# Running the first token block alone and first, gathering part of the expert rows early, and turning the up projection round

## The chip, the cores and the metric

One core of a Trainium2 chip runs the kernel. The metric is the device time of one execution in microseconds; lower is better.

## The reference

One decoder block over 512 tokens of width 2048, in float32: a mixer (one input projection, half of it causal spatial gating in chunks of 128 tokens, half of it attention over a window of 128 tokens with sinks, one output projection) and then a channel mixer that picks, for every token and each of 8 heads, 16 of 16384 experts.

```python
h = rmsnorm(x, norm1_g);  z = h @ w_in
a_out = chunked_spatial_gating(gelu(zu), gelu(zv), ...)      # chunks of 128 tokens
b_out = sliding_window_attention(zq, zk, zvv, attn_sinks)    # window of 128
x = x + concatenate([a_out, b_out]) @ w_out
h2 = rmsnorm(x, norm2_g)
# peer(h2): 8 heads, top 16 of 128 x 128 product keys
q = h2 @ w_query;  s1, s2 = q1 @ sub_keys[0].T, q2 @ sub_keys[1].T
experts, gates = top16(top16(s1) + top16(s2)), softmax       # 128 experts for a token
a = gelu(einsum('cd,chkd->chk', h2, expert_down[experts]))
x = x + einsum('chk,chkd->cd', gates * a, expert_up[experts])
out = rmsnorm(x, norm_f_g)
```

## The kernel before

All matrix products are float32 made of three float32r products: an operand is split into a high part (a cast) and a low part (the rest), and `mm3` issues high x high, high x low and low x high. Weights come as 1 MiB chunks [128, 2048] in the order of their use. `Stream` loads them from SP into two buffers (`wraw`), casts each half on ScalarE (ACT) to `whi` and subtracts it on VectorE (DVE) or, where `on_pool` says so, on GpSimd (POOL) to `wlo`; each half is a *piece*, four pieces fit, and a piece is made two pieces ahead of its use. The request for a chunk stands in SP's queue behind the second split of the chunk that held its buffer.

The program runs in this order, and every engine takes its instructions in the order in which they are written:

1. The mixer for all four blocks of 128 tokens: `kT` and `vT`, eight tiles of queries, `v` by rows, eight tiles of `u` with attention and gating spread between (`attend`, `gate`), `mix`, the output projection (`project`, chunks of `wout`), second norm.
2. Queries of the channel mixer (`wq`) and the choice of experts (`choose`: top 16 on VectorE), spread by `fill`, a queue of small jobs of which every `tick` takes some.
3. The experts. The first three blocks (`TD` = 384 tokens) are computed densely, against all 16384 experts: `down` steps (128 experts each, h2 against a chunk of `down`, 48 matmuls of 384 columns, weights stationary) and `up` steps (eight groups of experts, 288 matmuls of 512 columns, the activations `gah`, `gal` stationary and the weights moving). What was not chosen has gate 0. The gates come from a table that is built with one-hot products (`table`, `quad`: tiles `eq`, `p`, `low`, `stage`) during the first 51 `down` steps (`OPEN`) and goes through DRAM (`g_dram`); activations of the first 56 steps go through `a_dram`. `make_ga` multiplies and splits them.
4. The fourth block is not dense: its 128 tokens' expert rows are gathered, 512 halves of 512 KB (one row of 4 KB for each token; indirect DMA from GpSimd, `fetch`, four buffers), and VectorE takes a dot product with each (`unit`, table down) or adds it with its weight (table up). These 512 units begin when `start_gather` runs, in the tenth tick after the 51 `down` steps, and are paced evenly over the rest.

The change rewrites the whole of this plan inside one function; the lines that a step of the prediction needs stand in the diff below.

## Time and profile before

| | us |
|---|---|
| runs | 3041.81, 3042.4, 3045.75; median 3042.4 |
| span of the profiled execution, first to last instruction | 3046.2 |
| TensorE busy | 2939.4 (96%) |
| VectorE busy | 2228.9 (73%) |
| ScalarE busy | 1095.9 (36%) |
| GpSimd busy | 1220.4 (40%) |
| DMA moved | 696.85 MB, 229 GB/s on average |

The stretches of the program on this time line: the first matmuls start at about 23 us; the mixer to the output projection ends at 582; queries and choice end at 786; the 51 `down` steps with the tables last from 786 to 1338; from there to the end come 77 `down` and 16 `up` steps, the first seven `up` steps nearly on end (1380 to 1852), with the gather beside them. A busy TensorE is not a full one: matmuls overlap, and what one costs is read from the distance of two starts.

### The profile page before, as it was taken

How to read it: one execution, taken by the hardware profiler on the slowest of the kernel's cores; microseconds unless marked ns; L12 is line 12 of the kernel's file. 1: busy time of each engine (PE TensorE's matmuls, PEld its weight loads, DVE VectorE, ACT ScalarE, POOL GpSimd, SP SyncE). 2: the span in 40 equal slices, each digit the busy share in tenths (PEclk: the TensorE clock that was granted, in tenths of full speed). 3: DMA queues.
4: the chain of work that ended last, by engine and by line, in shares of the span. 5: the costliest groups of instructions: out<-in, count | busy, mean ns of one | idle time of the engine just before them, and what ended most of it. 6: DMA issues, size and time to landing. Idle time of an engine off the chain costs nothing.

```text
span 3046.2 us, 38888 instructions
## 1 busy us (share of the span) xinstructions
PE 2939.4 (96%) x15021; PEld 2623.7 (86%) x15021; DVE 2228.9 (73%) x3266; ACT 1095.9 (36%) x1699; POOL 1220.4 (40%) x754
## 2 busy tenths in 40 slices
PE   7999999999989888999999999999999999999998
PEld 6888878799989888898788889898998989899896
DVE  3125642359998999967888887878888888888864
ACT  3244432222236655643323233232322323232333
POOL 2132100334435555633344344545445454554522
PEclk9999999999999999999999999999999999999999
DMA  5221242322334444569888888998989898898953
GB/s 188 90 82 57 70 166 88 120 83 84 110 115 159 155 168 160 195 250 350 302 312 333 328 304 316 328 328 311 331 312 339 312 336 314 318 340 314 338 212 132
DMA packets 193866, 696.85 MB, mean 229 GB/s; under 512 B 16528, under 2 KB 81296, under 8 KB 148240
## 3 DMA queue, kind: packets, MB, share of 16 engines
q1 hardware_dynamic: 104960, 378.04, 35.0%
q0 software_dynamic: 73728, 268.47, 24.4%
q10 hardware_dynamic: 14992, 47.86, 4.0%
q8 instruction: 118, 1.93, 0.3%
q14 instruction: 68, 0.56, 0.1%
HBM read 650.78 MB, written 43.52 MB: 228 GB/s over the span
## 4 chain that ended last, share of the span: by engine, by line
PE 49%; DVE 20%; issue 15%; POOL 10%; ACT 3%; DMA 2%; ACTq 0%; POOLq 0%; SPq 0%; DVEq 0%
POOL row L879 10%; PE dn L133 5%; PE acc L131 5%; PE dn L132 5%; PE dn L131 5%; PE acc L133 5%; PE acc L132 5%; PE up L132 5%; PE up L131 5%; PE up L133 5%; DVE wlo L112 4%; DVE stage L754 3%; DVE eq L719 2%; DVE cand L572 1%; PE tr L339 1%
## 5 line engine op out<-in xcount | busy, mean ns | idle before, releaser
L110 ACT CAST whi<-wraw 128x1024 fp32r<-128x1024 f32 x628 | 639.7, 1048 | 738.9 <-DMA wraw<-in_up 321.1
L112 DVE TENSOR_TENSOR wlo<-wraw,whi 128x1024 fp32r<-128x1024 f32 x550 | 719.5, 1312 | 252.9 <-ACT whi L110 251.9
L133 PE MATMUL dn<-h2d,wlo 128*128 128x384 f32 x2048 | 695.2, 339 | 28.8 <-DVE wlo L112 25.6
L131 PE MATMUL dn<-h2d,whi 128*128 128x384 f32 x2048 | 694.0, 339 | 8.4 <-ACT whi L110 8.4
L132 PE MATMUL dn<-h2d,whi 128*128 128x384 f32 x2048 | 692.3, 338 | 0.0
L131 PE MATMUL up<-whi,gah 128*128 128x512 f32 x1536 | 598.9, 390 | 3.2 <-DVE acc L978 3.0
L132 PE MATMUL up<-wlo,gah 128*128 128x512 f32 x1536 | 598.8, 390 | 3.0 <-DVE wlo L112 3.0
L133 PE MATMUL up<-whi,gal 128*128 128x512 f32 x1536 | 598.3, 390 | 0.0
L879 POOL DMA_INDIRECT row<-in_down_rows,idx x256 | 367.6, 1436 | 492.0 <-DVE row L894 470.2
L879 POOL DMA_INDIRECT row<-in_up_rows,idx x256 | 364.7, 1425 | 366.4 <-DVE half_row L901 345.5
L133 PEld LDWEIGHTS dn<-h2d,wlo 128*128 128x128 f32 x2048 | 388.1, 190 | 37.3 <-DVE wlo L112 33.1
L112 POOL TENSOR_TENSOR wlo<-wraw,whi 128x1024 fp32r<-128x1024 f32 x78 | 194.9, 2519 | 559.0 <-ACT whi L110 559.0
L131 PEld LDWEIGHTS dn<-h2d,whi 128*128 128x128 f32 x2048 | 388.5, 190 | 10.5 <-ACT whi L110 10.1
L132 PEld LDWEIGHTS dn<-h2d,whi 128*128 128x128 f32 x2048 | 388.4, 190 | 0.4
L131 PEld LDWEIGHTS up<-whi,gah 128*128 128x128 f32 x1536 | 288.8, 188 | 65.9 <-DVE acc L978 4.7
L132 PEld LDWEIGHTS up<-wlo,gah 128*128 128x128 f32 x1536 | 288.6, 188 | 63.3 <-DVE wlo L112 4.4
L133 PEld LDWEIGHTS up<-whi,gal 128*128 128x128 f32 x1536 | 288.8, 188 | 60.0
L901 DVE SCALAR_TENSOR_TENSOR half_row<-row,wgt,half_row 128x1024 f32<-128x1024 f32 x256 | 328.9, 1285 | 14.8 <-DMA row<-in_up_rows,idx 11.7
L894 DVE SCALAR_TENSOR_TENSOR row<-row,half_row 128x1024 f32<-128x1024 f32 x256 | 307.1, 1215 | 18.9 <-DMA row<-in_down_rows,idx 17.3
L722 POOL TENSOR_TENSOR p<-eq,gT 128x1024 fp32r<-128x1024 bf16 x96 | 236.2, 2468 | 206.9 <-DVE eq L719 196.0
L978 DVE TENSOR_TENSOR acc<-up,acc 128x512 f32<-128x512 f32 x192 | 129.3, 690 | 92.5 <-PE up L133 92.3
L951 ACT ACTIVATE aa<-dn 128x384 f32<-128x384 f32 x72 | 35.4, 492 | 348.2 <-PE dn L133 348.2
(194 smaller groups left out, 3441.6 us busy)
## 6 DMA issues: line engine op xcount, KB each, us to landing
wraw<-in_down SPq DMA_DIRECT2D x128, 1024.0 KB
wraw<-in_up SPq DMA_DIRECT2D x128, 1024.0 KB
wraw<-in_win SPq DMA_DIRECT2D x26, 1024.0 KB
g_dram<-stage ACTq DMA_DIRECT2D x24, 1024.0 KB
g<-g_dram SPq DMA_DIRECT2D x32, 768.0 KB
wraw<-in_wout SPq DMA_DIRECT2D x16, 1024.0 KB
wraw<-in_wq SPq DMA_DIRECT2D x16, 1024.0 KB
aa<-a_dram SPq DMA_DIRECT2D x56, 192.0 KB
```

Source lines behind the costliest of these rows:

```text
L110: self.nc.scalar.copy(hi, src)
L112: eng.tensor_sub(lo, src, hi.bitcast(F32))
L131: nc.tensor.matmul(ps, wh, xh, start=start, stop=False)
L132: nc.tensor.matmul(ps, wh, xl, start=False, stop=False)
L133: nc.tensor.matmul(ps, wl, xh, start=False, stop=stop)
L719: nc.vector.tensor_tensor(eq, iota[:, None, :].to_broadcast([P, 4, P]), t[:, 1, four, None].to_broadcast([P, 4, P]), op=OP.is_equal)
L722: nc.gpsimd.tensor_tensor(p2, eq[:, :, None, :].to_broadcast([P, 4, 2, P]), hl[:, four, :, None].to_broadcast([P, 4, 2, P]), op=OP.mult)
L754: nc.vector.tensor_tensor(stage[h][:, :, o:o + 4], ps[:, :, 0, k].rearrange("p t k -> p k t"), low[:, :, k].rearrange("p t k -> p k t"), o ...
L879: nc.gpsimd.indirect_dma_start(out=t, out_offset=None, in_=src, in_offset=bass.IndirectOffsetOnAxis(ap=idx[:, j, h:h + 1], axis=0))
L894: nc.vector.scalar_tensor_tensor(t, t, 1.0, half, op0=OP.mult, op1=OP.mult, accum_out=dots[:, j, h:h + 1])
L901: nc.vector.scalar_tensor_tensor(half, t, wgt[:, j:j + 1], half, op0=OP.mult, op1=OP.add)
L978: nc.vector.tensor_add(y, ps[b], y)
```

## The change

The first block of tokens becomes the gathered one, and runs through the whole mixer and its choice of experts before the other three begin. The weights of the mixer and of `wq` are therefore read and split twice: `wrow` (26 chunks), `wout` and `wq` (16 each) for block 0, tokens stationary and weights moving, and then again for blocks 1 to 3. The last 64 of the 512 tokens (`EX`) are gathered too, as 64 x 2 partitions with 256 further units; the dense part falls from 384 to 320 tokens. The gather is a `Flow` that `mm3` itself steps, at a rate for each part of the program (one unit in 2300 ns, 4500 ns, 3600 ns of matmul time, then evenly). Running sums and inputs of the gather pass through DRAM (`h_dram`, `y_dram`, `x_dram`). The `up` steps now keep the weights stationary and move the 320 activations, so that the result is transposed and has to be turned at the end (`rows_out`). Which splits GpSimd makes follows a rule of the piece's number.

```diff
-TD = ND * P
+TL = ND * P
+EX = 64
+TD = TL - EX
...
+    def step(self, ns):
+        if not self.q:
+            return
+        self.credit = min(self.credit + ns * self.rate, 3.0)
+        while self.q and self.credit >= 1.0:
+            self.credit -= 1.0
+            self.q.popleft()()
...
-    chunks = [a["win"][i] for i in range(26)]
-    chunks += [a["wout"][i] for i in range(16)]
-    chunks += [a["wq"][i] for i in range(16)]
+    lead = [a["wrow"][i] for i in range(26)] + [a["wout"][i] for i in range(16)]
+    lead += [a["wq"][i] for i in range(16)]
+    chunks = lead + [a["win"][i] for i in range(10)] + [a["wrow"][i] for i in range(10, 18)]
+    chunks += [a["win"][i] for i in range(10, 18)]
+    chunks += [a["wout"][i] for i in range(16)] + [a["wq"][i] for i in range(16)]
...
-    W.on_pool = [range(0, 4), range(20, 36), range(2 * 42 - 2, 2 * 70)]
+    def on_pool(p):
+        if p < 84:
+            return p % 4 == 1 and p > 4
+        if p < 116:
+            return p % 4 != 0
+        if p < 200:
+            return p % 2 == 0
+        if p < 232:
+            return p % 4 != 0
+        if p < 232 + 2 * OPEN:
+            return p % 2 == 0
+        return p % 3 == 0
...
+    def row_group(x, width, evac, every=2, budget=0.0):
+        ps = acc_tile()
+        n = 1024 // width
+        for i in range(KT // n):
+            hi, lo = W.get()
+            for k in range(n):
+                kt = i * n + k
+                c = slice(k * width, (k + 1) * width)
+                mm3(ps[:, :width], (x[0][:, kt, :], x[1][:, kt, :]), (hi[:, c], lo[:, c]),
+                    kt == 0, kt == KT - 1)
+            if kt == KT - 1:
+                evac(ps)
+            after_piece(every, budget)
...
+    counts = (P, EX)
+    units = [(i, src, h, j) for i, n in enumerate(counts) for src in (n_down, n_up)
+             for h in range(2) for j in range(n)]
...
-            ps = [late["ps"].tile([P, 512], F32, name="up", bufs=4) for _ in range(ND)]
+            ps = [late["ps"].tile([P, TD], F32, name="up", bufs=4) for _ in range(4)]
...
-                hi, lo = ga[CB * c + j]
-                mm3(ps[b], (hi[:, t], lo[:, t]), (w[0][:, k], w[1][:, k]), j == 0, j == CB - 1)
+            def multiply(m, j, w):
+                k = (j % 2) * 512 + m * P
+                x = ga[CB * c + j]
+                mm3(ps[m], (w[0][:, k:k + P], w[1][:, k:k + P]), x, j == 0, j == CB - 1)
...
+            w = [W.get(1), W.get(2)]
+            for m in range(4):
+                for j in range(4, 8):
+                    multiply(m, j, w[j // 2 - 2])
+                y = accT[:, 4 * q + m, :]
+                if c == 0:
+                    nc.scalar.copy(y, ps[m])
+                else:
+                    nc.vector.tensor_add(y, ps[m], y)
...
+    def pace():
+        left = sum(2 * 24 for k, i in order if k == "d" and i >= OPEN)
+        left += sum(384 for k, i in order if k == "u")
+        flow.rate = len(flow.q) / (left * TD * COL_NS - 40e3)
```

The order of instructions at three places. First VectorE while the tables are built; `eq` and `p` are one-hot tiles, `stage` takes the products, `wlo` is the split of a piece, `row` a gathered tile. Before:

```order
L754 TENSOR_TENSOR stage<-tr,low 128x64x4 x2
L719 TENSOR_TENSOR eq<-iota,eT 128x512
L112 TENSOR_TENSOR wlo<-wraw,whi 128x1024
L754 TENSOR_TENSOR stage<-tr,low 128x64x4 x2
L719 TENSOR_TENSOR eq<-iota,eT 128x512
L726 TENSOR_TENSOR p_9886<-iota,eT 128x512
```

and now:

```order
L972 TENSOR_TENSOR eq<-iota,eT 128x512
L119 TENSOR_TENSOR wlo<-wraw,whi 128x1024
L614 SCALAR_TENSOR_TENSOR row,dots_85<-row,half_row 128x1024
L1007 TENSOR_TENSOR stage<-tr,low 128x64x4 x2
L972 TENSOR_TENSOR eq<-iota,eT 128x512
L1007 TENSOR_TENSOR stage<-tr,low 128x64x4 x2
L972 TENSOR_TENSOR eq<-iota,eT 128x512
L979 TENSOR_TENSOR p_10398<-iota,eT 128x512
```

The dot products with gathered rows (`L614`), which stood behind the tables, now stand among them, some ninety in the 51 `down` steps, and one split of a chunk's two is left on VectorE.

Second GpSimd in the tail, between two stretches of the same length. Before, only requests for gathered rows stand there:

```order
L879 DMA row_22803<-in_up_rows,idx_3983 128x1024
L879 DMA row_22843<-in_up_rows,idx_3983 128x1024
L879 DMA row_22875<-in_up_rows,idx_3983 128x1024
L879 DMA row_22878<-in_up_rows,idx_3983 128x1024
L879 DMA row_22920<-in_up_rows,idx_3983 128x1024
```

and now:

```order
L601 DMA row_15787<-in_up_rows,idx0_79 128x1024
L119 TENSOR_TENSOR wlo_15816<-wraw_15675,whi_15815 128x1024
L601 DMA row_15829<-in_up_rows,idx0_79 128x1024
L601 DMA row_15856<-in_up_rows,idx0_79 128x1024
L601 DMA row_15880<-in_up_rows,idx0_79 128x1024
L119 TENSOR_TENSOR wlo_15887<-wraw_15739,whi_15886 128x1024
L601 DMA row_15912<-in_up_rows,idx0_79 128x1024
```

Every third piece is split here, and the requests for rows queue with the splits.

Third TensorE at the start of an `up` step. Before, with 512 weight columns moving past 128 tokens:

```order
L131 MATMUL up_11380<-whi_11293,gah_11127 128x512
L132 MATMUL up_11380<-wlo_11294,gah_11127 128x512
L133 MATMUL up_11380<-whi_11293,gal_11128 128x512
L131 MATMUL up_11381<-whi_11293,gah_11127 128x512
L132 MATMUL up_11381<-wlo_11294,gah_11127 128x512
```

and now, with 320 tokens moving past 128 weight columns:

```order
L143 MATMUL up_12728<-gah_12465,whi_12641 128x320
L144 MATMUL up_12728<-gal_12466,whi_12641 128x320
L145 MATMUL up_12728<-gah_12465,wlo_12642 128x320
L143 MATMUL up_12729<-gah_12465,whi_12641 128x320
L144 MATMUL up_12729<-gal_12466,whi_12641 128x320
```

The two operands changed places; an `up` step has 384 matmuls of 320 columns in place of 288 of 512.

## Rows read from the trace of the kernel before

**Rows 1.** Stretches: length; busy (count) of PE, PEld, DVE, ACT, POOL; clock; DMA share, GB/s.

```profile
56.30:388.90 332.60, 331.62 (x1685) 267.88 (x1685) 130.08 (x231) 126.80 (x263) 70.56 (x32) 1.00 0.23 80
388.90:581.90 193.00, 186.21 (x820) 149.03 (x818) 71.25 (x82) 56.43 (x89) 7.05 (x9) 1.00 0.34 126
581.90:786.50 204.60, 198.87 (x1119) 188.40 (x1120) 144.32 (x566) 57.62 (x78) 84.60 (x36) 0.99 0.25 88
786.50:1337.60 551.10, 497.66 (x2845) 480.44 (x2844) 510.77 (x730) 301.83 (x583) 290.62 (x118) 0.97 0.45 156
...
1337.60:3046.20 1708.60, 1690.52 (x8305) 1505.78 (x8303) 1352.95 (x1641) 529.50 (x657) 749.67 (x529) 1.00 0.86 310
...
1778.00:2908.00 1130.00, 1129.25 (x5715) 1027.46 (x5714) 932.56 (x1064) 342.85 (x413) 561.88 (x396) 1.00 0.90 323
```

**Rows 2.** Timeline of TensorE in three places: start, length, line, operation, tiles, shape.

```profile
23.12 0.28 PE L133 MATMUL acc<-hT,wlo 128*128 128x256 f32 x1
23.23 0.28 PE L131 MATMUL acc<-hT,whi 128*128 128x256 f32 x1
...
1860.26 0.34 PE L133 MATMUL dn<-h2d,wlo 128*128 128x384 f32 x1
1860.43 0.34 PE L131 MATMUL dn<-h2d,whi 128*128 128x384 f32 x1
...
1500.17 0.39 PE L131 MATMUL up<-whi,gah 128*128 128x512 f32 x1
1500.40 0.39 PE L132 MATMUL up<-wlo,gah 128*128 128x512 f32 x1
```

**Rows 3.** Groups of instructions of VectorE and GpSimd in the table stretch, 786.5 to 1337.6.

```profile
L112 DVE TENSOR_TENSOR wlo<-wraw,whi 128x1024 fp32r<-128x1024 f32 x80 | 141.3, 1766 | 28.1 <-ACT whi L110 27.7
L754 DVE TENSOR_TENSOR stage<-tr,low 128x256 f32<-128x256 f32 x192 | 107.8, 607 | 3.9 <-ACT low L751 3.9
L719 DVE TENSOR_TENSOR eq<-iota,eT 128x512 bf16<-128x512 f32 x96 | 94.9, 998 | 0.0
L726 DVE TENSOR_TENSOR p<-iota,eT 128x512 fp32r<-128x512 f32 x33 | 29.3, 888 | 0.0
...
L722 POOL TENSOR_TENSOR p<-eq,gT 128x1024 fp32r<-128x1024 bf16 x96 | 236.2, 2468 | 206.9 <-DVE eq L719 196.0 <-PE tr L738 7.8 <-PE tr L702 3.2
L112 POOL TENSOR_TENSOR wlo<-wraw,whi 128x1024 fp32r<-128x1024 f32 x22 | 54.5, 2501 | 60.5 <-ACT whi L110 60.5
```

**Rows 4.** Groups of instructions of VectorE from 1380 to 2908.

```profile
L112 DVE TENSOR_TENSOR wlo<-wraw,whi 128x1024 fp32r<-128x1024 f32 x371 | 452.6, 1220 | 14.2 <-ACT whi L110 13.6 <-issue 0.6
L901 DVE SCALAR_TENSOR_TENSOR half_row<-row,wgt,half_row 128x1024 f32<-128x1024 f32 x247 | 317.4, 1285 | 14.7 <-DMA row<-in_up_rows,idx 11.7 <-ACT half_row L892 0.4
L894 DVE SCALAR_TENSOR_TENSOR row<-row,half_row 128x1024 f32<-128x1024 f32 x256 | 307.1, 1215 | 18.9 <-DMA row<-in_down_rows,idx 17.3 <-ACT half_row L892 1.4
L978 DVE TENSOR_TENSOR acc<-up,acc 128x512 f32<-128x512 f32 x180 | 121.1, 690 | 78.4 <-PE up L133 78.2
L864 DVE TENSOR_TENSOR gal<-aa,gah 128x384 fp32r<-128x384 f32 x116 | 64.9, 559 | 69.1 <-ACT gah L863 69.1
```

**Rows 5.** Stretches as in rows 1, around one chunk that SP requests at 198.30.

```profile
198.30:199.20 0.90, 0.90 (x5) 0.72 (x5) 0.87 (x2) 0.00 (x0) 0.00 (x0) 1.00 0.00 0
199.20:203.00 3.80, 3.80 (x18) 3.04 (x17) 2.34 (x4) 1.69 (x3) 0.00 (x0) 1.00 0.80 276
```

**Rows 6.** Timelines of SP's queue and of ScalarE: a loaded chunk's request, its casts.

```profile
1524.78 6.03 SPq L100 DMA_DIRECT2D wraw<-in_up  x2
...
1532.51 2.00 ACT L110 CAST whi<-wraw 128x1024 fp32r<-128x1024 f32 x2 [6.24 <-DMA wraw<-in_up]
```

**Rows 7.** Stretches as in rows 1, two of the best 20 us of DMA.

```profile
1460.00:1480.00 20.00, 20.00 (x90) 16.54 (x89) 16.25 (x24) 4.11 (x4) 10.61 (x8) 1.00 1.02 406
...
1660.00:1680.00 20.00, 20.00 (x90) 16.57 (x89) 16.06 (x24) 4.11 (x4) 9.44 (x7) 1.00 1.02 401
```

**Rows 8.** The page's costliest groups: GpSimd's requests for rows.

```profile
L879 POOL DMA_INDIRECT row<-in_up_rows,idx x256 | 364.7, 1425 | 366.4 <-DVE half_row L901 345.5 <-DVE wlo L112 7.5 <-DVE row L894 5.9
```

More of the change, by code (lines that the diff above doesn't have):

```diff
@@ L110, in make @@
             self.nc.scalar.copy(hi, src)
-            eng = self.nc.gpsimd if any(p in r for r in self.on_pool) else self.nc.vector
+            eng = self.nc.gpsimd if self.on_pool(p) else self.nc.vector
             eng.tensor_sub(lo, src, hi.bitcast(F32))
@@ new lines, in block_kernel @@
+    row_group(hT0, 512, lambda ps: nc.scalar.activation(v0[:, 512:], ps, AF.Gelu))
+    rest = layernorm(plab, v0, lng0, lnb0)
+    nc.scalar.dma_start(gbc, bcast(a["norm2_g"], D))
+    rest()
+    row_group(hT0, 512, lambda ps: nc.scalar.activation(u0[:, :512], ps, AF.Gelu))
+    soon.append([lambda: gate_rows(0)])
+    soon.append([lambda: turn_gated(0)])
+    row_group(hT0, 512, lambda ps: nc.scalar.activation(u0[:, 512:], ps, AF.Gelu), every=1)
+    while soon:
+        for f in soon.popleft():
+            f()
@@ new lines, in block_kernel, with decode_first @@
+    for g in range(4):
+        qr = pdec.tile([P, 512], F32, name="qr")
+        if g:
+            soon.append([lambda b=g: x_norm(b)])
+            soon.append([lambda b=g: x_turn(b)])
+        row_group(hT0, 512, lambda ps, qr=qr: nc.scalar.copy(qr, ps), 1, 2.0)
+        if g < 3:
+            x_in(g + 1)
+        soon.extend(score_first(g, qr))
+    plc.release()
+    choice0, steps = decode(temps0, key0, top0, pos0, gate_g[0])
+    def decode_first():
+        for step in steps:
+            fill.add(*step)
+        fill.add(0.4, lambda: gather_index(choice0, choice0["ef"][:, 2, :], idx[0]))
+        fill.add(0.0, lambda: start_job(0))
@@ L400, in block_kernel @@
     plan = [[] for _ in range(40)]
     start = 0
-    for b in range(NB):
-        heads = attention(b)
+    for b in range(1, NB):
+        heads = attention(pa, b, qT, (b - 1) * P)
         for hf in range(2):
@@ L458, in block_kernel @@
     for g in range(GROUPS):
-        rest = layernorm(g) if g < NB else None
+        rest = layernorm(pa, vg[:, g, :], lng, lnb) if g < ND else None
         column_tile(lambda ps, g=g: nc.scalar.activation(uT[:, g, :], ps, AF.Gelu), attend)
@@ L599, in block_kernel @@
         cols = [acc_tile() for _ in range(4)]
-        rows = acc_tile()
-        def dense(i, hi, lo):
+        for i in range(8):
+            hi, lo = W.get()
             for k in range(2):
@@ L763, in quad @@
             return f
-        return turn, [quad(n) for n in range(32)]
+        return turn, [quad(n) for n in range(min(P, TD - b * P) // 4)]
     tick_no = 0
@@ L805, in start_tables @@
             if b + 1 < ND:
-                choice, steps = decode(b + 1)
+                choice, steps = decoding(b + 1)
                 next_turn, next_quads = table(b + 1, choice)
@@ L1006, in up @@
                             a_load(nxt + 7)
-                tick(weight(c, q))
-    o_rows = out.rearrange("(b p) d -> b p d", p=P)
+                tick()
+            if last and q:
+                rows_out(q - 1)
+            if nxt is not None and q == 3:
+                for j in range(4, 6):
+                    make_ga(nxt + j)
+            w = [W.get(1), W.get(2)]
+            for m in range(4):
+                for j in range(4, 8):
[3 more added lines that the diff above has]
+                    nc.scalar.copy(y, ps[m])
+                else:
+                    nc.vector.tensor_add(y, ps[m], y)
+            if nxt is not None and q == 3:
+                for j in range(6, 8):
+                    make_ga(nxt + j)
+            tick()
+            tick()
+        if last:
+            rows_out(3)
+        for j in range(CB):
+            del ga[CB * c + j]
     def open_last():
```

1030 lines of the change are left out of this document (576 added, 454 removed).

## The prediction, made before the result was known

> **What bounds the kernel now.** I read the stretches first [rows 1]. From 1337.6 us to the end, 1708.6 us, TensorE is busy 1690.5 us; in the stretch from 1778 to 2908 us inside it, it is busy 1129 of 1130 us, with VectorE at 932.6 (83%) and DMA at 0.90. The reader should see one full engine and nothing else near its end. How full is told by starts, not by busy time [rows 2]: with 256 moving columns one float32r matmul starts every 0.12 us, with 384 every 0.173, with 512 every 0.227; that is about 0.42 ns a column plus 12 ns. The tail's 77 down and 16 up steps are 3696 x 0.173 + 4608 x 0.227 = 1685 us, so only 23 us of the 1708.6 are anything else.
>
> The table stretch (786.5 to 1337.6 us) is another kind: 2448 matmuls x 0.173 and 384 products x 0.118 are 469 us, but it takes 551; VectorE is busy 510.8 of them (93%) [rows 1]. Its splits take 1766 ns there [rows 3] against 1220 ns in the tail [rows 4]. The three stretches of the mixer before it are TensorE's again with friction: 56.3 to 581.9 us takes 525.6 for 1920 x 0.227 = 436 us of matmuls (1.20 times), 581.9 to 786.5 takes 204.6 for 768 x 0.173 + 192 x 0.227 = 176 us (1.16 times) [rows 1, 2].
>
> **What the change takes away.** The dense part goes from 384 to 320 tokens. A matmul of 320 columns lies between the measured ones: 0.42 x 320 + 12 = 146 ns, 145.5 taken. Down: 6144 x (173 - 145.5) = 169 us less. Up: 4608 x 0.227 = 1046 us becomes 6144 x 0.1455 = 894, 152 less. Together 321 us of matmul time, all behind one another on the full engine. Weight loads don't stand against it: at 256 columns they already hide behind 0.12 us [rows 2]. The mixer's columns are the same in number, only cut otherwise.
>
> **What it adds.** 256 gathered rows (64 tokens, two per expert row and table half), 58 MiB of weights read and split a second time, the splits' move to GpSimd, and a chain for one block ahead of all. I go through the program by stretches.
>
> *Lead* (block 0 alone, 42 chunks of `wrow` and `wout`, then 16 of `wq`). Each 1 MiB chunk now feeds 12 matmuls x 0.227 = 2.7 us; before it fed 8 us or more. Supply can't follow. There are two `wraw` buffers; SP asks for a chunk when the second split of the one before last is done. A chunk asked for at 198.3 us begins to move at 199.2 and is through at 203.0: 4.7 us [rows 5]. Then two casts (2.0 us [rows 6]) and, where the second split is on GpSimd (`p % 4 == 1`), 2.5 us [rows 3]: 9.3 us for a turn that yields two chunks, 4.65 each. In `wq` both splits of every second chunk are on GpSimd: 4.7 + 1.0 + 5.0 = 10.7, 5.3 each. So 42 x 4.65 + 16 x 5.3 = 280 us, with 22 us ahead of the first matmul (23 now [rows 2]), 8 for the block's layernorm and second norm, where four split pieces are all that is ahead, and 22 for `kT` and `vT`, where 4 pieces of 4.2 us carry 6 us of choices each: 332 us. Bounds: 260, if transfer and split of the two buffers overlap better (3.4 a chunk); 380, if attention's ACT steps delay the casts every time, or TensorE, idle 40% of the time, falls to 1.2 of its 2.4 GHz (12 x 0.45 = 5.4 us a chunk).
>
> *Blocks 1 to 3, queries to `wout`*: 768 x 0.173 + 864 x 0.227 = 329 us, x 1.20 = 395. VectorE: three quarters of its 201 us of before, 137 gathered rows x 1.25 us [rows 4] and the first block's decoding (26 us, a quarter of the table stretch's decoding) make 348, so it fits, with little over. 12 us for the norm's turn. `wq`: 768 x 0.173 = 133, x 1.16 = 154. Bounds 500 and 630 for these together, 561 taken.
>
> *Tables*: TensorE falls to 2448 x 0.1455 + 320 x 0.118 = 394 us, but it wasn't the bound. VectorE: stage, eq and p 232 us x 80/96 quads = 193 [rows 3]; its other 137 us (510.8 - 232 - 141.3 [rows 1, 3]) stay about as they are, a block less to decode but more choices left over, 140; 91 gathered rows x 1.3 = 118; 51 splits at the contended 1766 ns = 90. Sum 541, at the same 93% 584 us. So this stretch gets 33 us **longer** although its matmuls shrink. Bounds 520 (splits at 1220 ns, 97% busy) and 640.
>
> *Tail*: 9840 x 0.1455 = 1432 us, 23 for what is over now, and 30 for DMA. The seven up steps that come first now take 56 us each in place of 87 and still move 8 MiB of weights, 20 gathered rows of 0.5 MB and 2.6 MB of `aa` and `g4`: 21.5 MB in 56 us, 385 GB/s. Now it is 310 on average, and 401 to 406 in its best 20 us at a full DMA share [rows 1, 7]. The price is 0 at 403, 77 us at 322; I take 30, nearer the best rows, since the queue never lacks requests there. VectorE: 502 rows x 1.26, 274 splits x 1.22, 240 sums and 256 steps of `make_ga` at about 0.49 (0.690 at 512 columns, 0.559 at 384 [rows 4]): 633 + 334 + 243 = 1210, 81%, as now. GpSimd: 502 requests x 1.43 [rows 8] and 137 splits x 2.5 = 1060, 71%. 1486 us.
>
> Sum: 332 + 561 + 584 + 1486 = 2963 us, against a span of 3046.2; the runs' median, 3042.4, lies 4 under that span, so 2960. Of 321 us of matmuls saved, 222 come in the tail (1708.6 - 1486), and 139 are given back ahead of it (1477 in place of 1337.6).
>
> **A row against a rule.** VectorE's split takes 1220 ns in the tail, where GpSimd only issues gathers [rows 4], and 1766 ns in the tables, where GpSimd's vector work fills 291 of 551 us [rows 3]. The change puts 137 GpSimd splits into the tail; its 343 us of 1486 are 23%, and in proportion VectorE's splits there would take 1220 + 546 x 23/53 = 1457 ns, 65 us more in all: 86% busy, nothing at the end. The Trainium skill ("SBUF — State Buffer", section "Who interferes with whom") says that a VectorE instruction with two SBUF inputs and a GpSimd instruction that reads SBUF lock each other out for a whole instruction. By that rule each pair that meets costs up to 2.5 us instead of a share, and the estimate of 65 us could be twice or three times as large. These sentences aside, the case is rival 3.
>
> **Rivals.** 1, *all of it hides*: the lead runs at 3.4 us a chunk (-72), the tables at their lower bound (-64), the tail with no DMA price (-30): 2797 us. For it: transfer and splits of the two buffers may overlap more than a turn in a row allows. Against: VectorE at 93% in the tables already. 2, *the weights' turn binds the tail*: a piece is needed every 3.5 us, two chunks every 14.0. Loaded, a chunk takes 7.7 us from request to cast (1524.8 to 1532.5 [rows 6]); with two casts and a GpSimd split 12.2. Should transfers slow to 10 us and GpSimd's split wait 1 us behind a gather, a turn is 15.5 us, 205 chunks x 0.75 = 154 us: 3114. It decides from 14.8 us on. Slower than before. For it: 215 MB of weights, 263 of rows and some 40 of the rest in 1486 us are 349 GB/s in place of 310; against: 406 is on record [rows 7]. 3, *the tail becomes like the tables*: if VectorE's splits take 1766 ns in the tail too, it is busy 1210 + 150 = 1360 of 1486 us, 92%, and in the tables that share went with 17% on top of the matmuls; half of that is 120 us: 3080. Against: 23% GpSimd work, not 53%. 4, *320 columns are no faster than 384*: 338 us back, 3300; the three measured spacings speak against it.
>
> **How the numbers follow.** Forecast (2900 to 3036) 0.49; rival 1 0.22; rival 2 0.13; rival 3 0.13; rival 4 0.03. A measurement of this kernel tells about 0.2%, 6 us. Faster 0.49 + 0.22 less 0.03 at the edge, 0.68; within 0.2% 0.05; slower 0.27. The range reaches down to 2820, near rival 1, and up to 3120, past rivals 2 and 3; the likeliest alone is 2900 to 3036.
>
> **What would show it.** Starts of `up` and `dn` matmuls 0.145 us apart; lead chunks asked for every 4.5 to 5.5 us with TensorE waiting on `wlo`; `kT` begun near 310 us, tables begun near 890 and 570 to 600 us long with VectorE above 90%; a tail of 1460 to 1520 us. The prediction is wrong if the lead keeps under 3.5 us a chunk, if the tables end before 1400 us, or if in the tail `dn` and `up` wait often for `wlo`.

## The result, and the profile after

The changed kernel takes 3314.6 us in the median (3304.95 to 3320.84, four runs) against 3044.1 (3041.81 to 3048.07, four runs) of the kernel before: 1.0887 times, with an interval of 1.0863 to 1.0911. It is slower by 8.9%, and outside the predicted range. The profiled execution spans 3303.2 us; the predicted sum for it was 2963.

The stretches after, as in [rows 1] (length; busy and count of PE, PEld, DVE, ACT, POOL; clock; DMA share, GB/s): block 0's mixer, its `wq`, blocks 1 to 3 up to `wq`, the tables, five `down` steps, six `up` steps, then nine rounds of eight `down` steps and one `up` step (the "pairs" below), and the last `up` step to the end. The tail is all from the end of the tables on.

```profile
21.90:231.80 209.90, 161.36 (x641) 116.15 (x641) 110.36 (x124) 105.36 (x150) 66.57 (x35) 0.91 0.57 216
231.80:357.70 125.90, 75.53 (x294) 56.10 (x294) 82.18 (x176) 54.30 (x67) 71.24 (x33) 0.80 0.49 184
357.70:1014.00 656.30, 588.84 (x3089) 523.45 (x3087) 501.38 (x954) 218.12 (x366) 369.93 (x253) 0.95 0.67 244
1014.00:1619.20 605.20, 461.38 (x2780) 438.74 (x2780) 577.13 (x881) 271.06 (x509) 398.26 (x231) 0.89 0.63 224
1619.20:1657.10 37.90, 36.52 (x242) 36.26 (x242) 27.35 (x30) 13.22 (x19) 17.50 (x13) 0.97 0.98 368
1657.10:2064.30 407.20, 363.34 (x2306) 353.13 (x2304) 322.68 (x360) 124.86 (x164) 215.64 (x154) 0.95 0.88 324
2064.30:3163.20 1098.90, 1044.78 (x6912) 1029.04 (x6913) 874.72 (x981) 352.51 (x438) 648.43 (x460) 0.98 0.88 324
3163.20:3303.20 140.00, 70.35 (x434) 66.78 (x432) 59.05 (x69) 35.78 (x62) 39.46 (x32) 0.75 0.43 153
```

The tables end at 1619.2 us in place of 1337.6, and the tail behind them, which was to be 222 us shorter, takes 1684 us in place of 1709. Its 9840 matmuls did become shorter. The timeline of TensorE in an `up` step shows both spacings that occur (start, length, line, operation, tiles, shape; in brackets the idle time before and what ended it):

```profile
1932.46 0.60 PE L143 MATMUL up<-gah,whi 128*128 128x320 f32 x1 [4.47 <-DVE accT L1213]
...
1935.19 0.47 PE L144 MATMUL up<-gal,whi 128*128 128x320 f32 x1
1935.46 0.47 PE L145 MATMUL up<-gah,wlo 128*128 128x320 f32 x1
...
1950.18 0.31 PE L144 MATMUL up<-gal,whi 128*128 128x320 f32 x1
1950.33 0.31 PE L145 MATMUL up<-gah,wlo 128*128 128x320 f32 x1
```

At 1950 us two starts lie 0.147 us apart, as good as the predicted 0.1455. The 9840 need 1446 us at that. After an idle time of 4.5 us they lie 0.27 apart: there the granted clock is at the lower of its two levels, 1.2 of 2.4 GHz, as the stretch around it shows (0.50 in the column of the clock):

```profile
1932.10:1938.90 6.80, 6.05 (x20) 5.28 (x21) 5.58 (x10) 1.52 (x3) 2.83 (x3) 0.50 0.94 340
```

So of 1684 us 238 are not matmuls at full speed: 68 in the six `up` steps (407.2 - 2304 x 0.147), 83 in the pairs (1098.9 - 6912 x 0.147), 65 in the last `up` step (122 of the last 140 us, for 384 matmuls), 18 behind it, 3 ahead. The waits of TensorE from 1665 to 3075 us say what was late (total, times, longest):

```profile
PE up L143 <- DVE accT L1213: 34.3, 32, 4.5
PE up L145 <- POOL wlo L119: 30.5, 16, 3.4
PE dn L145 <- POOL wlo L119: 9.7, 10, 2.4
PE dn L143 <- ACT whi L117: 6.4, 2, 5.1
```

VectorE's sums (`accT`, which free the accumulators) and GpSimd's splits. What held VectorE up is in its groups of the same stretch (busy, mean ns, idle before and its releaser), with GpSimd's below:

```profile
L626 DVE SCALAR_TENSOR_TENSOR half_row<-row,wgt,half_row 128x1024 f32<-128x1024 f32 x324 | 415.7, 1283 | 73.0 <-DMA row<-in_up_rows,idx 70.7
L119 DVE TENSOR_TENSOR wlo<-wraw,whi 128x1024 fp32r<-128x1024 f32 x241 | 368.9, 1535 | 73.1 <-ACT whi L117 71.4 <-PE up L145 1.5
L614 DVE SCALAR_TENSOR_TENSOR row<-row,half_row 128x1024 f32<-128x1024 f32 x128 | 153.9, 1214 | 45.9 <-DMA row<-in_down_rows,idx 35.9 <-ACT half_row L613 9.4
...
L119 POOL TENSOR_TENSOR wlo<-wraw,whi 128x1024 fp32r<-128x1024 f32 x120 | 289.3, 2411 | 68.2 <-issue 42.4 <-ACT whi L117 16.5 <-PE up L145 6.2
```

Against [rows 4]: a split takes 1535 ns in place of 1220, and VectorE stands 107 us on gathered rows that have not landed (70.7 + 35.9), where it stood 29 (11.7 + 17.3); everything behind a late row in its queue is late too. In the last `up` step it stands on another load (timeline):

```profile
3190.58 2.29 DVE L1279 TENSOR_TENSOR yf<-yf,xf 128x2048 f32<-128x2048 f32 x1 [21.12 <-DMA xf<-x_dram]
...
3230.08 2.28 DVE L1295 TENSOR_TENSOR xf<-xf,yf 64x2048 f32<-64x2048 f32 x1 [11.31 <-DMA xf<-x_dram]
```

### The profile page after: what moved, and what is told of

The parts are those of the page before. It is cut to its first block, busy times and chain, and to the rows that moved or that the text cites. A ratio compares the mean times of both kernels' runs of the same rounds, so it can differ in the third digit from the quotient of the medians.

```text
span 3303.2 us, 44165 instructions
## 1 busy us (share of the span) xinstructions
PE 2805.8 (85%) x16701; PEld 2622.6 (79%) x16701; DVE 2559.9 (77%) x3575; ACT 1181.9 (36%) x1782; POOL 1828.9 (55%) x1219
## 5 line engine op out<-in xcount | busy, mean ns | idle before, releaser
L119 POOL TENSOR_TENSOR wlo<-wraw,whi 128x1024 fp32r<-128x1024 f32 x297 | 732.1, 2467 | 327.6 <-ACT whi L117 272.6
L145 PE MATMUL dn<-h2d,wlo 128*128 128x320 f32 x2048 | 652.3, 318 | 78.0 <-POOL wlo L119 54.4
L143 PE MATMUL up<-gah,whi 128*128 128x320 f32 x2048 | 652.8, 319 | 70.4 <-DVE accT L1213 35.1
L145 PE MATMUL up<-gah,wlo 128*128 128x320 f32 x2048 | 650.4, 318 | 40.5 <-POOL wlo L119 34.0
L143 PE MATMUL dn<-h2d,whi 128*128 128x320 f32 x2048 | 647.0, 316 | 6.4 <-ACT whi L117 6.4
L144 PE MATMUL up<-gal,whi 128*128 128x320 f32 x2048 | 646.3, 316 | 0.0
L144 PE MATMUL dn<-h2d,whi 128*128 128x320 f32 x2048 | 645.1, 315 | 0.0
L614 DVE SCALAR_TENSOR_TENSOR row<-row,half_row 128x1024 f32<-128x1024 f32 x384 | 460.5, 1214 | 120.2 <-DMA row<-in_down_rows,idx 108.3
L626 DVE SCALAR_TENSOR_TENSOR half_row<-row,wgt,half_row 128x1024 f32<-128x1024 f32 x380 | 487.5, 1283 | 83.9 <-DMA row<-in_up_rows,idx 81.4
L143 PEld LDWEIGHTS up<-gah,whi 128*128 128x128 f32 x2048 | 397.4, 194 | 82.8 <-ACT whi L117 35.9
L145 PEld LDWEIGHTS up<-gah,wlo 128*128 128x128 f32 x2048 | 396.6, 194 | 50.2 <-POOL wlo L119 40.4
L144 PEld LDWEIGHTS up<-gal,whi 128*128 128x128 f32 x2048 | 397.5, 194 | 0.0
```

Of the source, the lines that this page charges most:

```text
L119: eng.tensor_sub(lo, src, hi.bitcast(F32))
L143: nc.tensor.matmul(ps, wh, xh, start=start, stop=False)
L144: nc.tensor.matmul(ps, wh, xl, start=False, stop=False)
L145: nc.tensor.matmul(ps, wl, xh, start=False, stop=stop)
L614: nc.vector.scalar_tensor_tensor(t, t, 1.0, half_row, op0=OP.mult, op1=OP.mult, accum_out=dots[i][:, j, h:h + 1])
L626: nc.vector.scalar_tensor_tensor(half_row, t, wgt[i][:, j:j + 1], half_row, op0=OP.mult, op1=OP.add)
```

## Experiments

Each run is compared with the 3314.6 us of the changed kernel; that kernel's own runs lie 16 us apart, so differences under 15 us are not read from the total. The columns behind the median are the stretches of each run's profile, as above. They vary too: in e5, e6 and e11, whose edits leave the pairs alone, the pairs take 1106 to 1115 us in place of 1098.9, so differences of some 16 us there are not read either. The medians of the kernel before beside them were 3042 to 3044.

| kernel | median | `kT` begins | to tables | tables | six `up` | pairs | last `up`, end |
|---|---|---|---|---|---|---|---|
| changed | 3314.6 | 357.7 | 656.3 | 605.2 | 407.2 | 1098.9 | 140.0 |
| e1 tail's splits on VectorE | 3279.4 | 359.4 | 661.9 | 607.9 | 395.8 | 1076.3 | 137.9 |
| e2 half the weights' bytes | 3273.8 | 358.1 | 662.1 | 605.5 | 390.7 | 1076.8 | 138.5 |
| e3 half the rows | 3213.0 | 358.2 | 661.1 | 604.8 | 380.0 | 1036.4 | 134.8 |
| e4 last sums later | 3297.6 | 358.7 | 657.8 | 606.0 | 408.0 | 1114.2 | 113.9 |
| e5 lead's splits on VectorE | 3290.3 | 332.8 | 659.3 | 603.4 | 407.9 | 1106.3 | 139.5 |
| e6 no early units | 3187.4 | 360.5 | 600.4 | 520.4 | 407.4 | 1108.8 | 143.7 |
| e7 no units of the last 64 | 3155.7 | 359.1 | 661.1 | 601.4 | 359.6 | 1016.4 | 121.7 |
| e8 six row buffers | 3287.7 | 357.7 | 661.6 | 603.9 | 398.8 | 1081.0 | 138.8 |
| e9 three edits | 3223.9 | 330.6 | 656.9 | 602.7 | 396.1 | 1075.5 | 110.3 |
| e10 no gather | 2976.2 | 358.5 | 590.6 | 520.8 | 337.9 | 1013.8 | 114.7 |
| e11 tables' splits on VectorE | 3325.3 | 360.0 | 657.3 | 615.4 | 405.4 | 1115.4 | 136.8 |
| e12 rows kept, sums whole | 3150.1 | 360.6 | 613.8 | 599.3 | 378.3 | 1032.9 | 132.7 |
| e13 rows whole, sums short | 3100.6 | 358.7 | 622.3 | 538.8 | 372.2 | 1036.8 | 132.0 |
| e14 four edits | 3207.9 | 332.0 | 659.5 | 602.8 | 388.0 | 1067.1 | 110.5 |

**GpSimd's splits.** First the tail without them:

```diff
         if p < 232 + 2 * OPEN:
             return p % 2 == 0
-        return p % 3 == 0
+        return False
```

> The changed kernel with every split of the tail on VectorE (no third on GpSimd). Its tail takes 1684 us from the end of the tables (1619) to the end, of which 9840 matmuls at 147 ns are 1446. Theory A (the DMA supply sets the tail's excess): within 15 us of 3315. Theory B (GpSimd's splits, late for TensorE and slowing VectorE's own splits to 1.53 us): TensorE's waits for GpSimd's wlo (17 + 15 + 10 us) vanish, VectorE's splits fall back to 1.22 us, and the time falls by 40 to 70 us. Theory C (VectorE's queue is too full): 124 more splits of 1.22 us less 77 us of recovered contention are 75 us more work there, and the time rises by 30 to 90 us.

Measured: 3279.4 us (1.0776 times the kernel before, 1.0749 to 1.0804), 35 less. Theory A is out as the only cause, C is out, and B has the sign with a smaller size than expected. VectorE's groups from 1665 to 3075 us:

```profile
L119 DVE TENSOR_TENSOR wlo<-wraw,whi 128x1024 fp32r<-128x1024 f32 x369 | 446.8, 1220 | 95.7 <-ACT whi L117 94.3 <-PE dn L145 0.9 <-PE up L144 0.5
L626 DVE SCALAR_TENSOR_TENSOR half_row<-row,wgt,half_row 128x1024 f32<-128x1024 f32 x335 | 429.5, 1282 | 27.5 <-DMA row<-in_up_rows,idx 25.8
```

The split is back at 1220 ns. What theory B had not named is the second row: the wait for rows falls from 70.7 to 25.8 us. No request stands behind a GpSimd split of 2.4 us any more, which fits it.

The same share of GpSimd splits in the tail of the kernel before:

```diff
-    W.on_pool = [range(0, 4), range(20, 36), range(2 * 42 - 2, 2 * 70)]
+    W.on_pool = [range(0, 4), range(20, 36), range(2 * 42 - 2, 2 * 70), range(218, 762, 3)]
```

> The kernel before, with one edit: every third split after the tables on GpSimd, as in the changed kernel. Theory B: VectorE's splits go from 1220 to about 1500 ns and TensorE waits for GpSimd's wlo, since a GpSimd split (2.5 us) stands behind gather requests (1.4 us): slower by 40 to 80 us, 3085 to 3125. Theories A and C: TensorE is the bound there with pieces needed every 4 us and VectorE gets lighter: within 10 us of 3044.

Measured: 3072.5 us (1.0089 times, 1.0062 to 1.0115), 30 more: below B's 40 to 80, above A's and C's 10. Two of VectorE's groups there, from 1380 to 2970 us:

```profile
L112 DVE TENSOR_TENSOR wlo<-wraw,whi 128x1024 fp32r<-128x1024 f32 x253 | 396.2, 1566 | 9.4 <-ACT whi L110 9.4
...
L894 DVE SCALAR_TENSOR_TENSOR row<-row,half_row 128x1024 f32<-128x1024 f32 x256 | 305.4, 1213 | 50.8 <-DMA row<-in_down_rows,idx 49.1 <-ACT half_row L892 1.4
```

and the whole stretch, in this run and then in the kernel before:

```profile
1380.00:2970.00 1590.00, 1572.96 (x7680) 1391.69 (x7680) 1278.98 (x1440) 477.55 (x576) 959.55 (x635) 1.00 0.88 316
```

```profile
1380.00:2970.00 1590.00, 1585.93 (x7796) 1414.19 (x7795) 1301.54 (x1581) 487.90 (x593) 728.24 (x508) 1.00 0.88 318
```

The split goes from 1220 to 1566 ns, the wait for rows of the first table half from 17.3 [rows 4] to 49.1 us, and VectorE is only 22.6 us lighter (1301.5 - 1279.0), although GpSimd spent some 306 us on 127 splits. Even that is an upper bound: the same 1590 us hold 116 matmuls less in b1, and the other work of VectorE that goes with them.

The tables, with all splits on VectorE:

```diff
         if p < 232 + 2 * OPEN:
-            return p % 2 == 0
+            return False
```

> The changed kernel with all splits of the 51 down steps on VectorE (half of them are GpSimd's now). Theory (the two engines slow each other there, so GpSimd's half saves VectorE little): 51 splits more at 1.2 to 1.5 us are 61 to 77 us, and eq (1341 ns back to 998, 27 us), p (15), oh (13) and the other splits (25) give about 80 back: the tables within 20 us of their 605. Rival (GpSimd's share is real relief): the tables 40 to 75 us longer.

Measured: tables 615.4 us in place of 605.2, as the theory had it; the total, 3325.3, does not differ by what can be told. Half of the splits taken from GpSimd raise VectorE's load by 8.6 us, 585.7 in place of 577.1:

```profile
1017.30:1632.70 615.40, 466.62 (x2780) 443.85 (x2779) 585.69 (x932) 271.27 (x509) 284.19 (x180) 0.88 0.62 220
```

because what stands beside them gets shorter. `eq` in the changed kernel's tables, then in this run's:

```profile
L972 DVE TENSOR_TENSOR eq<-iota,eT 128x512 bf16<-128x512 f32 x80 | 106.4, 1341 | 0.0
```

```profile
L972 DVE TENSOR_TENSOR eq<-iota,eT 128x512 bf16<-128x512 f32 x80 | 71.0, 899 | 0.0
```

**Bytes, and late rows.** Half of each weight chunk from piece 334 on:

```diff
-            self.nc.sync.dma_start(self.raw[i], self.chunks[i])
+            w = 2048 if i < 167 else 1024
+            self.nc.sync.dma_start(self.raw[i][:, :w], self.chunks[i][:, :w])
...
-            src = self.raw[p // 2][:, (p % 2) * 1024:(p % 2 + 1) * 1024]
+            h = p % 2 if p < 334 else 0
+            src = self.raw[p // 2][:, h * 1024:(h + 1) * 1024]
```

> The changed kernel with half of each weight chunk loaded from the end of the tables on (both pieces of a chunk are split from its first half, so the tail multiplies by wrong weights); instructions of all engines stay. Theory A: the weights' bytes were late, so the gaps of TensorE in the tail (67 us in the six up steps on end, 82 us in the pairs) go to under 50 together and the time falls by 80 to 130 us, to about 3210. Theories B and C: GpSimd and VectorE do the same work, so at most 25 us less.

Measured: 3273.8 us, 41 less, under A's 80 and over the others' 25. 205 chunks lost half a MiB each, 107 MB, and gave back 39 of the 151 us in the `up` steps and pairs. The weights' bytes are a part, not the cause.

Half of the rows from unit 256 on:

```diff
+            if u >= 256 and u % 2:
+                rows_at[u] = rows_at[u - 1]
+                return
             t = pg.tile([P, D // 2], F32, name="row", bufs=4)
```

> The changed kernel where, from unit 256 on, every second gathered row isn't fetched but its neighbour's tile is used twice (so the sums are wrong): half of the later requests and bytes of the gather are gone, VectorE's operations all stay. Theory A: bytes fall by 134 MB, time falls by 60 to 130 us. Theory B: GpSimd has 256 requests of 1.14 us less in its queue, its splits come earlier, but contention stays: 20 to 50 us less. Theory C: VectorE's waits for rows (about 110 us in the tail) go, which is up to 60 us.

Measured: 3213.0 us, 102 less, with 20 us of 83 left in the pairs. 134 MB are gone, against 107 in e2, for two and a half times its gain, inside theory A's 60 to 130. But the edit also takes 256 requests out of GpSimd's queue and VectorE's waits for rows with them, so it doesn't tell bytes from late rows; the next run does.

Two more row buffers, lent from tiles that are used only at the end:

```diff
+    def use_late(u):
+        return "p" in late and u < 700 and list(held.values()).count("yf") < 2
...
+            if use_late(u):
+                t = late["p"].tile([P, D], F32, name="yf", bufs=2)[:, :D // 2]
+            else:
+                t = pg.tile([P, D // 2], F32, name="row", bufs=4)
```

> The changed kernel with six buffers for gathered rows in place of four, from the end of the tables to unit 700 (the two come from tiles that are free until the end). Theory (rows are late for VectorE because a request waits for the unit four before it, and then behind a GpSimd split): VectorE's waits for rows in the tail, about 107 us, fall below 50, and the time falls by 25 to 60 us. Rival (the rows' bytes are late, whatever the distance of the request): waits above 80 us, the time within 12 us of 3315.

Measured: 3287.7 us (1.0806, 1.0778 to 1.0833), 27 less, and the waits for rows all but vanish. One of VectorE's groups, 1665 to 3075 us:

```profile
L644 DVE SCALAR_TENSOR_TENSOR half_row<-row,wgt,half_row 128x1024 f32<-128x1024 f32 x235 | 301.2, 1282 | 12.1 <-DMA row<-in_up_rows,idx 10.4
```

That is as the theory had it: the rows were late because the request came late, not because their bytes were too many. Only 27 us come of some 95, though. TensorE still waits 29 us for `accT` and 28 for GpSimd's `wlo` in that stretch, where it waited 34 and 31, and VectorE's splits take 1624 ns in place of 1535. Most of VectorE's standing on rows was not on TensorE's path by itself.

**Places.** The last sums, loaded where they were and taken up a quarter of an `up` step later:

```diff
+        def rest():
+            nc.vector.tensor_add(y, y, x)
...
+        late["rest"] = rest
...
+            if last and q == 1:
+                late["rest"]()
+            if last and q == 2:
+                flow.drain()
+                finish_last()
+            if last and q == 3:
+                late["rest"]()
```

> The changed kernel with the last part put in another order: the sums of the first block and of the last 64 tokens are still loaded at the same place, but VectorE takes them up a quarter of the last up step later, so that it doesn't stand on those loads with the splits behind it. The last up step takes 122 us with 56 us of matmuls. Theory: VectorE's waits of 21 and 11 us for xf, with the splits queued behind them, are on the path: 35 to 55 us less. Rival (the end is bound by the chunks, which come late behind 5 MB of other loads on SP's queue): under 15 us less.

Measured: 3297.6 us, 17 less; the end itself falls by 26 (140.0 to 113.9). Half of the expected 35 to 55, and between the two theories: the kernel without gather has an end of 114.7 as well, so what remains there is not the gather's. The turned result and the last norms stand there; no run takes them apart.

```diff
         if p < 84:
-            return p % 4 == 1 and p > 4
+            return False
         if p < 116:
-            return p % 4 != 0
+            return False
```

> The changed kernel with all splits of the lead (42 chunks of wrow and wout, 16 of wq) on VectorE. It takes 336 us now, 5.0 and 7.1 us a chunk. Theory: the turn of two buffers sets it, and a GpSimd split (2.5 us against 1.2) is the longest link after the transfer: 4.0 to 4.5 us a chunk, 50 to 90 us less. Rival: the choices, the attention and the norms on VectorE bind the lead, and more splits there lengthen it: 0 to 40 us more.

Measured: `kT` begins at 332.8 in place of 357.7 us, the total falls by 24. GpSimd's splits were a link of the lead's turn, but a smaller one than thought.

```diff
-    flow.rate = 1.0 / 2300.0
+    flow.rate = 0.0
...
         if i == 0:
-            stage_in(0, 0)
+            first = 2 * P
+            nc.gpsimd.memset(wgt[0], 0.5)
```

> The changed kernel without the first block's 256 units of dot products (left out of the computation, all weights 0.5) and with no gather before the end of the tables; the tail keeps 512 units, as it has now some 530. Theory: 228 early units stand in VectorE's queue ahead of what TensorE waits for, so the blocks 1 to 3 (656 us now) fall to 575 to 620 and the tables (605 us) to 500 to 550, which is 90 to 180 us less in all. Rival: the doubled weights and GpSimd's splits and one-hot products set these stretches: at most 40 us less.

Measured: 3187.4 us, 127 less: 56 between `kT` and the tables, 85 in the tables, as the theory had it.

```diff
-            if b == ND - 1:
-                steps = [*steps, (0.5, last_tokens(choice))]
...
-            fetch(u + 4)
+            if u + 4 < 4 * P:
+                fetch(u + 4)
```

> The changed kernel without the 256 units of the last 64 tokens (they are left without their experts), the other units spread over the tail. Theory: the tail's excess is the gather's (row waits on VectorE, requests and splits on GpSimd, DMA): the pairs fall from 1099 to about 1020 us, the six up steps from 407 to about 370, the end by 20: 110 to 170 us less. Rival: the excess comes from the up step's new order (sums late in VectorE's queue): 30 to 60 us less. In both cases, less than the 321 us of matmuls that the change from 384 to 320 columns saves means that the 64 tokens alone are a gain and the lead is the loss.

Measured: 3155.7 us, 159 less, all in the tail; the pairs stand at 1016.4 us, the bare matmuls. So the new order of the `up` step costs nothing by itself, and that rival falls. Gathering the 64 tokens costs 159 us, all in the tail, where the change from 384 to 320 columns takes 239 us of matmuls away (1685 - 1446). By this sum that half of the change is a gain; no run makes it alone. In this run 248 units are left in the tail, VectorE's splits still take 1619 ns there, and it no longer stands on rows (1665 to 3030 us):

```profile
L119 DVE TENSOR_TENSOR wlo<-wraw,whi 128x1024 fp32r<-128x1024 f32 x255 | 410.3, 1619 | 148.5 <-ACT whi L117 148.5
L626 DVE SCALAR_TENSOR_TENSOR half_row<-row,wgt,half_row 128x1024 f32<-128x1024 f32 x239 | 306.1, 1281 | 0.6
```

So longer splits alone don't make TensorE wait.

**The whole gather, and its two halves.**

```diff
     def start_job(i):
+        return
```

> The changed kernel without any gathered unit (the experts of the first block and of the last 64 tokens are left out; choices, tables and all dense work stay). Theory (the gather beside it is what the blocks 1 to 3, the tables and the tail pay for): the tables end at about 1480 us as in the run without early units, the six up steps take 340 to 360, the rest to the last up step 1016 to 1030, the end about 100: 2970 to 3010, only 35 to 75 us under the kernel before, which gathers 512 units. Rival (half of the excess is the weights' second reading, GpSimd's splits and the new up order): 3050 to 3120.

Measured: 2976.2 us (0.9785 times the kernel before, 0.9769 to 0.9802), inside the theory's 2970 to 3010. From `kT` to the last `up` step (stretches as above):

```profile
358.50:949.10 590.60, 564.42 (x3087) 507.96 (x3086) 313.65 (x662) 216.86 (x364) 195.98 (x85) 0.99 0.34 123
949.10:1469.90 520.80, 439.72 (x2780) 427.46 (x2779) 464.62 (x650) 270.12 (x508) 314.07 (x130) 0.90 0.43 156
...
1506.70:1844.60 337.90, 337.90 (x2306) 337.90 (x2305) 181.76 (x238) 123.55 (x161) 81.08 (x33) 1.00 0.57 197
1844.60:2858.40 1013.80, 1013.80 (x6914) 1013.80 (x6913) 423.66 (x483) 348.89 (x432) 236.53 (x96) 1.00 0.45 161
```

The tail is bare matmuls. The gather costs 338 us, and it costs them everywhere: by the spans 66, 84, 69, 85 and 25 us in the five long stretches from `kT` to the end (to the tables, tables, six `up` steps, pairs, end).

For e12, seven of eight fetches are left out and VectorE's work stays:

```diff
+            if u % 8:
+                rows_at[u] = rows_at[u - 1]
+                return
```

> The changed kernel where only every eighth gathered row is fetched and its tile used eight times (sums wrong): VectorE's work of the gather stays whole, seven eighths of its bytes and GpSimd requests are gone. Between the changed kernel (3315) and the one without gather (2976) lie 339 us. If the gather's price is VectorE's time, the run keeps most of it: 3200 to 3280. If it is bytes, requests and late rows, it gives most back: 3010 to 3090.

and for e13 the fetches stay and VectorE reads 64 of 1024 columns:

```diff
+                s = slice(0, 64)
-                nc.vector.scalar_tensor_tensor(t, t, 1.0, half_row, op0=OP.mult, op1=OP.mult,
-                                               accum_out=dots[i][:, j, h:h + 1])
+                nc.vector.scalar_tensor_tensor(t[:, s], t[:, s], 1.0, half_row[:, s], op0=OP.mult,
+                                               op1=OP.mult, accum_out=dots[i][:, j, h:h + 1])
```

> The opposite: every row is fetched as in the changed kernel and VectorE still takes each one up in turn, but reads 64 of its 1024 columns (sums wrong): some 0.15 us in place of 1.25. If the price is VectorE's time: 3000 to 3080. If it is bytes, requests and late rows: 3200 to 3300. If both runs give back most, each alone would fit beside the rest and only both together don't.

Measured: 3150.1 and 3100.6 us, both between the two answers. VectorE's work with one eighth of the fetches is worth 174 us over the kernel without gather, the fetches with short sums 124, together 298 of 338; the remaining 40 arise only where both meet, above all in the pairs (1033 and 1037 alone, 1099 together, 1014 without). The tables are VectorE's (599 and 539 of 605). e12's and e13's pairs:

```profile
1988.80:3021.70 1032.90, 1020.22 (x6915) 1016.50 (x6914) 844.91 (x981) 352.95 (x437) 299.24 (x143) 1.00 0.52 183
```

```profile
1930.30:2967.10 1036.80, 1020.32 (x6915) 1015.70 (x6914) 513.52 (x981) 352.30 (x437) 651.03 (x462) 1.00 0.92 344
```

VectorE 82% busy, or DMA at 344 GB/s: each alone costs TensorE some 20 us there. Late rows alone cost little as well. In e13 VectorE stands 258 us on them from 1565 to 2960 us, more than twice the 107 of the changed kernel:

```profile
DVE half_row L628 <- DMA row<-in_up_rows,idx: 187.0, 101, 5.2
...
DVE row L615 <- DMA row<-in_down_rows,idx: 70.7, 36, 6.5
```

The counterpart in the kernel before:

```diff
-        for u in range(len(units)):
-            fill.paced.append(unit(u))
```

> The kernel before without its 512 gathered units (the fourth block's experts are left out). In its tail TensorE waits for nothing that the gather makes late, 23 us in 1709 are not matmuls: 3020 to 3042, so those 512 units cost at most 25 us, where the changed kernel pays 339 for 768. Rival (the gather costs the same per unit in both plans, 0.44 us): about 2820.

Measured: 3036.4 us (0.9976, 0.9967 to 0.9986), inside the expected 3020 to 3042. There 512 units in the tail cost 8 us. In the changed kernel the run with as many units in the tail is e6, and it lies some 194 us over e10 there (407.4 - 337.9, 1108.8 - 1013.8 and 143.7 - 114.7). Without the units of the kernel before VectorE is busy 762 us of the stretch behind the tables, with them 1353 [rows 1], and TensorE is none the better for it:

```profile
1333.30:3031.00 1697.70, 1686.76 (x8305) 1505.11 (x8304) 762.36 (x871) 529.02 (x650) 17.36 (x17) 1.00 0.46 154
```

**Versions with the same result.** e1, e4 and e5 together, and then with e8 as well:

> The three earlier edits that keep the result, together: the tail's splits on VectorE (35 us less alone), the lead's splits on VectorE (24 less), the last sums taken up a quarter later (17 less). If they act in different stretches they add: 3239, between 3230 and 3250. If the end's gain is only what the tail's splits leave idle: 3255 or more.

> The four edits that keep the result and gained alone: splits of the tail and of the lead on VectorE, the last sums later, six row buffers (35, 24, 17 and 27 us; the first three together 91). If the row buffers still help when no GpSimd split stands ahead of a request: 3195 to 3205. If the splits were what made rows late: 3215 to 3225. Neither reaches the 3044 of the kernel before.

Measured: 3223.9 us, below the expected 3230 to 3250 (91 less, where the three alone give 76), and 3207.9 (1.0536, 1.0512 to 1.0561), 16 less again and between the two answers. The row buffers still help without GpSimd splits, with about half of their 27 us. No version that keeps the result came under the 3044 of the kernel before.

## Why the prediction was wrong

The sum missed by 340 us of span (3303 - 2963). What failed is the price of the gather: the prediction counted its work in the tables, where VectorE was full, and took it as free in blocks 1 to 3 and, but for 30 us of DMA, in the tail, because VectorE and GpSimd had time left there. Without the gather the program spans 2973 us (e10), 330 less, so the gather is worth nearly the whole miss. That 2973 lies so near 2963 is partly chance: the lead is 48 us longer than its term, and the tables, whose term had 118 us of gathered rows in it, 63 shorter. By the prediction's own steps:

1. **320 columns, right.** 0.147 us against 0.1455; the tail's matmuls 1446 us against 1432. Rival 4 is out; that its 3300 lies nearest to the result is luck.
2. **Lead, too short by 48** (`kT` at 357.7, predicted near 310), which makes the term 380, its upper bound. (The turn of 4.7 + 2.0 + 2.5 us is 9.2, not 9.3: 2 us in all.) 42 chunks took 210 us, 5.0 each against 4.65. Most of the rest is `wq`, whose 16 chunks took 113 us of the 126 in that stretch, 7.1 each against 5.3. The norms and transposes of blocks 1 to 3, which are written between those chunks, were in no term: from 245 to 330 us TensorE waits 10.5 us for a norm (`xt`) and 7.1 for the transposed parts (`hT`), both VectorE's. GpSimd's splits are 25 us of the 48 (e5). The granted clock was 0.91 and 0.80 in the two stretches, which the prediction had in its upper bound alone; what it cost there is not told apart.
3. **Blocks 1 to 3, too short by 73** (656 against 22 + 561). The failed step is "so it fits, with little over": VectorE's time was counted, and a free rest taken to mean that nothing waits. Without gather the stretch takes 590.6, near the term; the early units cost 56 to 66 (e6, e10), 23 with VectorE's work and few fetches, 32 with the fetches and short sums (e12, e13).
4. **Tables, too short by 21** (605 against 584), with VectorE busy 577 of 605 us (95%, predicted 93). That VectorE binds held (e12); `eq` and `p`, taken over at their old 998 and 888 ns, took 1341 and 1425, 42 us more; without GpSimd's new splits `eq` takes 899 (e11).
5. **Tail, too short by 198** (1684 against 1486), the main miss. The term allowed 23 us for what was over before and 30 for DMA. It counted VectorE at 81% and GpSimd at 71% and took both as free, as 83% had been free before [rows 1]. Measured over matmuls: 238 us, of which the gather is 179 (69 + 85 + 25, e10); the rest is the last `up` step and the end, 58 over their matmuls without the gather too. What failed is reading a busy share as cover. VectorE was busy 80% of the pairs and TensorE waited; in the kernel before 83% cost nothing. The prediction's own sign of being wrong came: 26 waits for GpSimd's `wlo`, 40 us, and beside them 34 us for `accT`. Three things changed that can turn the same work into waits: a piece is used up in 3.5 us where it took 4.1 (18 matmuls of 0.227 us), requests share a queue with splits, and a late row holds up splits and `accT` behind it. With the last two all but gone, e14 still has some 50 us over e10 in the six `up` steps and 53 in the pairs.
6. **DMA in the up run.** The prediction's bound was 77 us at 322 GB/s, 0 at 403, and it took 30. Measured: 324 GB/s and 68 us over. That is the bound's number but not its reason: in the run without gather the same steps need no extra time, with half the weights' bytes they still have 52 us over, with VectorE's work and one eighth of the fetches 40 (e12), and with all the bytes and short sums 34, at 355 GB/s (e13). So the 30 was not far off for the bytes; what the term lacked is VectorE's work beside them.

Of the rivals, 3 came nearest in mechanism (splits at 1535 ns, its price 1766) and is a small part of the miss: taking GpSimd's splits out of the tail returned 35 us of 340. Rival 2, the weights' turn, is bounded by e2: with half the transfer a turn would be well under the 14.0 us that it may take, and 41 us came back.

**The rule weighed against the row.** Splits in the tail were estimated at 1457 ns by proportion, 65 us in all. They took 1535, and `aa` (L1123) 677 ns against 484 in e1: (1535 - 1220) x 241 + (677 - 484) x 114 = 98 us, one and a half times the estimate. The Trainium skill ("SBUF — State Buffer", section "Who interferes with whom") names VectorE instructions with two SBUF inputs as those that contend with GpSimd instructions that read SBUF; the trace agrees, in that splits, `aa` and `eq` stretched, while the gather's dot products, whose second input lies in PSUM, stayed at 1207 to 1219 ns in every stretch. One row does not follow it: `gal`, with two SBUF inputs as well, took 492 ns both here and in e1, though it went from 559 to 719 in b1; which instructions meet is not shown. And the stretch was not the price: with splits at 1619 ns the pairs ran bare (e7).

By place, against the spans of the kernel before: the tables begin 228 us later (1014.0 against 786.5), of which the gather is 66 and the rest the lead, since block 0 needs 336 us of its own and blocks 1 to 3 still take 656 up to the tables, where four blocks took 787 from the start. The tables take 54 us more, with 84 of gather in them. The tail takes only 25 less, because 179 of gather, and 34 more over the matmuls at the end (57 in e10, 23 before), are set against 239 of matmuls saved. Counted in units, 264 stand ahead of the tail and cost 150 us, 504 in the tail and cost 179; with 248 in the tail (e7) it is some 31, so the price is far from even.

What stays open: how the 40 us that arise only with both halves of the gather divide between DMA's load and VectorE's queue, how the lead's 5.0 us a chunk splits beyond GpSimd's part, and what makes 512 units in the tail cost 194 us here and 8 before, beyond the splits' 35. The faster use of pieces is argued, not shown: no run changes it alone. A rival that no run tests is the number of accumulators. A quarter of an `up` step now fills all four `up` buffers, where it filled three of four before, so that none is spare while VectorE adds up `accT`. TensorE's waits for these sums were 3.0 us in the kernel before (1380 to 2970 us) and still 34.5 in e14 (1665 to 3075 us):

```profile
PE up L131 <- DVE acc L978: 3.0, 3, 1.8
```

```profile
PE up L143 <- DVE accT L1237: 34.5, 33, 4.2
```

## What to carry to other kernels

Work beside a bound engine is free only as long as its queue is never late, and a busy share of 80% doesn't say that: look for what stands in the same in-order queue, and how soon the bound engine needs it. When the plan around such work changes, price it again: 512 units in the tail went from 8 us to some 194. A run without the work at all, and one with each half of it, tell its price before it is spread further. Handing work to GpSimd is worth what VectorE gets rid of, net: measure it, since 51 splits on GpSimd were worth 9 us of VectorE here.

## What the runs showed of the hardware

Three things were unexpected. GpSimd's splits gave VectorE nearly nothing: at most 22.6 us for 306 us of GpSimd's time (b1), 8.6 us for 124 (e11). An idle time of 4.5 us on TensorE was followed by matmuls 0.27 us apart, in a stretch of 6.8 us at a granted clock of 0.50; 253 of the 9216 matmuls from 1657 to 3163 us started at that level, which at 0.12 us each makes 30 of the 151 us of excess. So a wait can cost more than its length, though not every one did: matmuls after an idle time of 2.8 us at 1739 us ran at the full clock. And two loads beside TensorE, VectorE's sums and the rows' fetches, that cost 19 and 23 us in the pairs each for itself (e12, e13) cost 85 together.
